# Loading x whole and gating on VectorE between the stages of a two-layer diffusion trunk on one Trainium2 core

## The chip, the cores and the metric

The kernel runs as one program on one core of a Trainium2 chip. The core's engines work side by side, each through its own list of instructions in a fixed order: TensorE (PE in the profile), VectorE (DVE), ScalarE (ACT), GpSimd (POOL), and SyncE (SP), which here issues the DMA transfers. An engine that has to wait for another holds up everything behind the waiting instruction in its own list. The metric is the device time of one execution in microseconds; lower is better.

## The reference, cut to what matters

The computation is two layers of a hybrid trunk over 640 tokens: 128 context tokens and 512 latent tokens, each of 1024 channels. What concerns the change is the end of each half of a layer:

```python
mix = (ga * ya + gb * yb + gc * yc) @ lp['w_o']
x = x + gt1 * rms_norm(mix, lp['g_post1'])

h2 = rms_norm(x, lp['g_pre2']) * (1 + sc2) + sh2
ffn = (jax.nn.silu(h2 @ lp['w_gate']) * (h2 @ lp['w_up'])) @ lp['w_down']
x = x + gt2 * rms_norm(ffn, lp['g_post2'])
```

So twice in a layer a product is normed over the channels (`rms_norm` divides by the root of the mean square), multiplied by a gate, and added to x; then x is normed again, scaled and shifted, and goes into the next products. The gate, scale and shift of a channel differ between context and latent tokens.

## The kernel before, in words

Activations lie with channels on the 128 partitions and tokens along the row: x is eight tiles (k = 0 to 7) of 128 by 640. Work on them is done in two halves of 320 tokens, h = 0 and h = 1. Half 0 holds all 128 context tokens and 192 latent ones, so a factor per channel needs two pieces there, of 128 and 192 columns (`SEGS`); half 1 is all latent and needs one piece of 320.

Products are in float32 by three matmuls: each operand is split into a high and a low part, and high by high, high by low and low by high are added up in PSUM. An item is one output block of 128 channels for one half: 24 matmuls where eight k-blocks are summed. Weights come by DMA into three raw buffers (`wraw`, 256 KB); ScalarE casts the high part (`wkh`, `whi`, `wk`; line 94) and VectorE subtracts it to get the low part (`wkl`, `wlo`, `wk`; line 95). A raw buffer is free again when VectorE's subtraction is done.

Four boundaries use `lin_res` (lines 459 to 510). I call them A (after w_o in layer 0), B (after w_down in layer 0, ahead of layer 1), C (after w_o in layer 1) and D (after w_down in layer 1, the end). At each:

1. Items of the product finish. For each, ScalarE squares the result into `sqt` (line 148), the squares are summed in `acc` by GpSimd and VectorE (line 152), and ScalarE multiplies the result by the gate into `y` (line 474; at B and D the tile is called `pt`, as it already holds a part of the sum, which VectorE adds first in line 471).
2. A matmul with ones (`ln`, line 157) sums `acc` over the channels, and ScalarE makes the factor `rs` by a logarithm and an exponential (lines 130 and 131).
3. For each k VectorE multiplies y by `rs` (line 498) and adds x (line 499). x was stored in memory and comes back in half tiles `xo` (line 496), which have three buffers. At D it already comes back whole (`xe`).
4. The squares of the new x are summed again: ScalarE squares, GpSimd adds k = 1 to 5, VectorE adds k = 6 and 7 (line 152); a second matmul with ones (`pn`) and a second `rs` follow.
5. `prenorm_apply` makes the next activations, a high and a low tile for each k (`h2h`/`h2l` at A and C, `hh`/`hl` at the start and at B). Half 0 does it in five instructions: VectorE multiplies by `rs` (line 175) and scales and shifts 128 columns (line 180), ScalarE does the other 192 (line 182) and casts the high part (line 183), VectorE subtracts (line 184). Half 1 needs three: VectorE (187), ScalarE (188), VectorE (189). The same function runs at the start of the kernel.

While this goes on for half 0, TensorE works on the items of half 1; while it goes on for half 1, TensorE works on the first items of the next stage with half 0's activations. The weights of both are kept, so each is split once. A scheduler sets the order of each engine's list before the run, from the program's dependences. Results of TensorE wait in three PSUM banks of the kind `l`; an item's bank is free when it has been read out, which at A and C for the gate item of the next stage means ScalarE's `fs` and VectorE's copy `fg` (line 429).

Of the kernel before, what the change touches and what calls it, by code (L numbers as in the profile page):

```python
# [8 lines left out]
F32 = mybir.dt.float32  # L9
F32R = mybir.dt.float32r  # L10
AF = mybir.ActivationFunctionType
ALU = mybir.AluOpType
AX = mybir.AxisListType

P = 128
# [15 lines left out]
NL, NB = 3, 5  # L31
NH_, NC_, NF_, NT_ = 16, 24, 16, 4
NWR, NW = 3, 3
NXO, NRR, NVW = 3, 3, 2

KEEP = ("C", "C", "C", "C", "E", None)
LEAD = ("C", "C", "C", "C", "E")
F1 = 14
# [14 lines left out]
def tile_trunk(ctx: ExitStack, tc: tile.TileContext, I: dict, O: list, layers=DEPTH):  # L53
# [7 lines left out]
    def slot(name, shape=(P, NT), dt=F32, tag="F"):  # L61
        n = {"H": NH_, "C": NC_, "F": NF_}[tag]
        return sb.tile(list(shape), dt, tag=tag, name=name, bufs=n)
# [2 lines left out]
        return slot(name, shape, dt, "C")  # L66

    def half(name, tag="T"):
        return sb.tile([P, HF], F32, tag=tag, name=name, bufs={"T": NT_, "acc": 3, "rs": 2, "xo": NXO}[tag])

    def lbank():
        return pp.tile([P, 512], F32, tag="l", name="l", bufs=NL)
# [7 lines left out]
    def hv(t, h):  # L80
        return t[:, h * HF:(h + 1) * HF]
# [86 lines left out]
    def prenorm_apply(src, h, r, gs, sh, hh, ks=range(KD)):  # L168
        for k in ks:
            if k:  # L170
                yield
            hi, lo = hh[k]
            t = half("hv")
            if h == 0:
                V.tensor_mul(t, hv(src[k], h), r)
                f = half("hf")
                for c0, c1, s in SEGS[h]:
                    g_, s_ = gs[:, k, s:s + 1], sh[:, k, s:s + 1]
                    if s:
                        V.tensor_scalar(out=f[:, c0:c1], in0=t[:, c0:c1], scalar1=g_, scalar2=s_, op0=ALU.mult, op1=ALU.add)  # L180
                    else:
                        A.activation(f[:, c0:c1], t[:, c0:c1], AF.Identity, scale=g_, bias=s_)
                A.copy(hv(hi, h), f)
                V.tensor_sub(hv(lo, h), f, hv(hi, h).bitcast(F32))
                continue
            s = 0
            V.scalar_tensor_tensor(out=t, in0=hv(src[k], h), scalar=gs[:, k, s:s + 1], in1=r, op0=ALU.mult, op1=ALU.mult)
            A.activation(hv(hi, h), t, AF.Identity, bias=sh[:, k, s:s + 1])
            V.scalar_tensor_tensor(out=hv(lo, h), in0=t, scalar=sh[:, k, s:s + 1], in1=hv(hi, h).bitcast(F32),
                                   op0=ALU.add, op1=ALU.subtract)  # L190

    def prenorm_half(src, h, gs, sh, hh):
        accs = prenorm_sum(src, h)
# [251 lines left out]
    def copy_ev(dst):  # L445
        def ev(h, pb):
            A.copy(hv(dst, h), pb)  # L447
        return ev

    def hslots(name, tag):  # L450
        return [(slot(f"{name}h{k}", dt=F32R, tag=tag), slot(f"{name}l{k}", dt=F32R, tag=tag)) for k in range(KD)]

# [3 lines left out]
        for k in range(KD):  # L456
            SY.dma_start(out=xd[k], in_=src[k])

    def lin_res(srcw, acts, ys, gs, keeps, part, after, end=False):

        accs = [[], []]
        n0 = KD - len(keeps)

        def ev(m):
            def f(h, pb):
                src = pb
                if part:
                    src = hv(ys[m], h)  # L470
                    V.tensor_add(src, src, pb)
                sumsq(accs[h], src, NSQ[m])
                for c0, c1, s in SEGS[h]:
                    A.mul(ys[m][:, c0:c1], src[:, c0 - h * HF:c1 - h * HF], gs[:, m, s:s + 1])
            return f

        def w(m):
            return srcw[:, m * P:(m + 1) * P]

        for m in range(n0):  # L480
            linear(w(m), acts, ev(m))
        bl = [wblocks(w(n0 + i), len(acts), k) for i, k in enumerate(keeps)]

        if end:
            xe = [slot("xe", tag="H") for _ in range(KD)]
            for k in range(KD):
                SY.dma_start(out=xe[k], in_=xd[k])

        def norm(h):
            r = half_rstd(accs[h], "ln")  # L490
            for k in range(KD):
                if end:
                    xo = hv(xe[k], h)
                else:
                    xo = half("xo", "xo")
                    SY.dma_start(out=xo, in_=hv(xd[k], h))
                E_ = G if end and k in ENDG else V
                E_.tensor_mul(hv(ys[k], h), hv(ys[k], h), r)
                E_.tensor_add(hv(ys[k], h), hv(ys[k], h), xo)
            yield from after(h)  # L500

        side = iter(())
        for h in range(2):
            for i, b in enumerate(bl):
                lin_half(b, acts, h, ev(n0 + i))
                next(side, None)
            drain(side)
            side = norm(h)
            next(side, None)
        return side  # L510
# [757 lines left out]
    for l in range(layers):  # L1268
# [33 lines left out]
        def fillc():  # L1302
# [8 lines left out]
            while len(yf) < 4:  # L1311
# [9 lines left out]
        ys = [cslot(f"y{k}") for k in range(KD)]  # L1321
        h2 = hslots("h2", "H")
        side = lin_res(I["w_o"][l], mix, ys, gsc[l][1], KEEP, False,
                lambda h: prenorm_half(ys, h, gsc[l][2], modT[l][:, 24:32, :], h2))
        mods = iter(())
        if l + 1 < layers:
            drain(load_rows(l + 1))
# [10 lines left out]
        if l + 1 < layers:  # L1338
            hh = hslots("h", "H")
            after = lambda h: prenorm_half(part, h, gsc[l + 1][0], modT[l + 1][:, 0:8, :], hh)  # L1340
        else:
            after = lambda h: out_half(part, h)
        side = lin_res(I["w_down"][l, F1 * P:], acts2, part, gsc[l][3], KEEP, True, after, l + 1 == layers)
        xs = part

    drain(side)
# [61 lines left out]
```

## Time and profile before

| | |
|---|---|
| median of 3 runs | 2819.4 us (2819.39 to 2822.23) |
| the profiled execution | 2820.49 us, of which the span is 2818.6 us |
| PE busy | 2724.1 us, 97% of the span |
| DVE busy | 1554.2 us, 55% |
| ACT busy | 1250.4 us, 44% |
| POOL busy | 114.2 us, 4% |
| mean granted clock of TensorE | 0.987 of full speed |

An engine's busy time is how long its instructions ran, overlaps counted once. With TensorE busy for 97% of the span, the time can only fall where TensorE waits or runs at a lower clock, and it rises wherever a change makes TensorE wait longer.

### The profile page before, as it was taken

The page shows a single profiled execution, that of the slowest core. Times are in us where ns is not written, and L with a number is a line of the kernel's source. Part 1 is how long each engine was busy: PE and PEld are TensorE (multiplying, and loading weights), DVE is VectorE, ACT ScalarE, POOL GpSimd, SP SyncE. Part 2 cuts the span into 40 slices and gives each one's busy share as a digit, 9 for nine tenths or more (in the row PEclk, how much of TensorE's full clock was granted, in tenths as well). Part 3 has the DMA queues.
Part 4 walks back from the last instruction along what each step waited for, and adds up shares of the span by engine and source line. Part 5 has one row for each costly group of instructions (what it writes and reads, how often), then busy time and mean ns, then how long its engine had stood idle before and what let it go on. Part 6 is the DMA issues. An engine that isn't in the chain of part 4 may idle for free.

```text
span 2818.6 us, 49773 instructions
## 1 busy us (share of the span) xinstructions
PE 2724.1 (97%) x19706; PEld 2594.3 (92%) x19706; DVE 1554.2 (55%) x3275; ACT 1250.4 (44%) x2863; POOL 114.2 (4%) x235
## 2 busy tenths in 40 slices
PE   7899999999999999999989999999999999999998
PEld 3898999999899899999978899999999989999997
DVE  4586566478743744324465865664778456442344
ACT  4432554466534533223455335434655354332333
POOL 1000000000001200000020000000000020000002
PEclk9999999999999999999999999999999999999999
DMA  8452355433464444444443323433233332222231
GB/s 244 77 85 46 79 100 117 85 71 84 155 161 137 146 132 144 128 159 143 132 115 75 78 49 79 104 98 82 65 98 118 94 108 92 76 74 77 75 119 64
DMA packets 401557, 293.45 MB, mean 104 GB/s; under 512 B 19318, under 2 KB 365228, under 8 KB 401324
## 3 DMA queue, kind: packets, MB, share of 16 engines
q1 hardware_dynamic: 401324, 290.28, 40.1%
q8 instruction: 154, 2.52, 0.3%
q14 instruction: 79, 0.65, 0.1%
HBM read 257.10 MB, written 33.11 MB: 103 GB/s over the span
## 4 chain that ended last, share of the span: by engine, by line
PE 78%; DVE 8%; DMA 8%; ACT 3%; issue 2%; SPq 0%; POOL 0%; DVEq 0%; ACTq 0%; POOLq 0%
PE l L363 21%; PE l L364 21%; PE l L365 21%; DMA rowb<-gd 3%; DMA wraw<-in_w_in_dram 2%; PE pm L324 1%; DVE wlo L95 1%; PE ptT L772 1%; PE po L782 1%; DVE tmpE L987 1%; DVE Tt L989 1%; PE sco L363 1%; DMA wm<-in_w_mod_dram 1%; PE scan L1068 1%; PE po L784 1%
## 5 line engine op out<-in xcount | busy, mean ns | idle before, releaser
L94 ACT CAST whi<-wraw 128x512 fp32r<-128x512 f32 (+1 forms) x540 | 331.2, 614 | 849.6 <-PE l L364 787.1
L95 DVE TENSOR_TENSOR wlo<-wraw,whi 128x512 fp32r<-128x512 f32 (+1 forms) x540 | 368.9, 684 | 537.4 <-ACT whi L94 507.8
L363 PE MATMUL l<-hh,whi 128*128 128x320 f32 x1856 | 592.0, 319 | 21.3 <-ACT padc L864 10.5
L365 PE MATMUL l<-hh,wlo 128*128 128x320 f32 x1856 | 584.4, 315 | 1.0 <-DVE wlo L95 1.0
L364 PE MATMUL l<-hl,whi 128*128 128x320 f32 x1856 | 584.4, 315 | 0.0
L363 PE MATMUL l<-h2h,whi 128*128 128x320 f32 x1248 | 387.7, 311 | 0.0
L364 PE MATMUL l<-h2l,whi 128*128 128x320 f32 x1248 | 385.7, 309 | 0.0
L365 PE MATMUL l<-h2h,wlo 128*128 128x320 f32 x1248 | 385.6, 309 | 0.0
L363 PEld LDWEIGHTS l<-hh,whi 128*128 128x128 f32 x1856 | 353.3, 190 | 28.9 <-ACT padc L864 11.8
L365 PEld LDWEIGHTS l<-hh,wlo 128*128 128x128 f32 x1856 | 353.4, 190 | 2.2 <-DVE wlo L95 1.2
L364 PEld LDWEIGHTS l<-hl,whi 128*128 128x128 f32 x1856 | 353.2, 190 | 2.1
L363 PEld LDWEIGHTS l<-h2h,whi 128*128 128x128 f32 x1248 | 234.6, 188 | 7.0 <-ACT fs L427 3.1
L364 PEld LDWEIGHTS l<-h2l,whi 128*128 128x128 f32 x1248 | 234.7, 188 | 0.0
L365 PEld LDWEIGHTS l<-h2h,wlo 128*128 128x128 f32 x1248 | 234.6, 188 | 0.0
L363 PE MATMUL l<-ah,whi 128*128 128x320 f32 x544 | 169.1, 311 | 0.0
L152 POOL TENSOR_TENSOR acc<-acc,sqt 128x320 f32<-128x320 f32 x88 | 88.1, 1001 | 1985.2 <-ACT sqt L148 1983.4
L365 PE MATMUL l<-ah,wlo 128*128 128x320 f32 x544 | 168.1, 309 | 0.0
L364 PE MATMUL l<-al,whi 128*128 128x320 f32 x544 | 167.9, 309 | 0.0
L363 PE MATMUL l<-rsh,whi 128*128 128x320 f32 x384 | 119.4, 314 | 0.0
L364 PE MATMUL l<-rsl,whi 128*128 128x320 f32 x384 | 118.4, 312 | 0.0
L365 PE MATMUL l<-rsh,wlo 128*128 128x320 f32 x384 | 118.2, 310 | 0.0
L363 PEld LDWEIGHTS l<-ah,whi 128*128 128x128 f32 x544 | 102.2, 188 | 2.2 <-ACT pt L447 1.7
(428 smaller groups left out, 5420.4 us busy)
## 6 DMA issues: line engine op xcount, KB each, us to landing
wraw<-in_w_in_dram SPq DMA_DIRECT2D x256, 256.0 KB, 4.3
wm<-in_w_mod_dram SPq DMA_DIRECT2D x80, 512.0 KB, 4.8
wraw<-in_w_gate_dram SPq DMA_DIRECT2D x88, 256.0 KB, 2.9
wraw<-in_w_up_dram SPq DMA_DIRECT2D x88, 256.0 KB, 3.1
wraw<-in_w_down_dram SPq DMA_DIRECT2D x80, 256.0 KB, 2.8
rowb<-gd SPq DMA_DIRECT2D x32, 320.0 KB, 9.4
mixo<-mixd SPq DMA_DIRECT2D x32, 320.0 KB, 3.4
wm<-in_w_mod_dram SPq DMA_DIRECT2D x32, 256.0 KB, 3.9
```

Of the source, the lines that this page charges most:

```text
L94: A.copy(hi, src)
L95: V.tensor_sub(lo, src, hi.bitcast(F32))
L152: (V if n == 2 else G).tensor_add(accs[0], accs[0], t)
L324: T.matmul(pm[32 * u:32 * u + 2, 0:256], lhsT=sc[:, k, :], rhs=w[:, u * 256:(u + 1) * 256], start=(n == 0), stop=(n == KD - 1))
L363: T.matmul(out, lhsT=wh, rhs=ah, start=first, stop=False)
L364: T.matmul(out, lhsT=wh, rhs=al, start=False, stop=False)
L365: T.matmul(out, lhsT=wl, rhs=ah, start=False, stop=last)
L772: T.transpose(pt[:, i, q * P:(q + 1) * P], sm_[q][:, kt * P:(kt + 1) * P], ident)
L782: T.matmul(po, lhsT=vh, rhs=th, start=(kt == 0), stop=False)
L784: T.matmul(po, lhsT=vh, rhs=tl, start=False, stop=(kt == 4))
L987: V.tensor_tensor(out=tv, in0=Tt[:, j + 1:32, j:j + 1].to_broadcast([P, n, j]), in1=Tt[:, j:j + 1, 0:j].to_broadcast([P, n, j]), op=ALU.mult)
L989: V.tensor_add(Tt[:, j + 1:32, 0:j], Tt[:, j + 1:32, 0:j], tv)
```

## The change

Three edits, all between the stages:

- x is loaded whole (eight transfers of 128 by 640) into the high tiles of the next activations, which are empty until `prenorm_apply` writes them; the half tiles `xo` are gone. The loads are issued right behind those of the kept weights.
- The gate is no longer applied when an item is read out. ScalarE only copies the product (or does nothing at B and D, where VectorE has already added it in place), and VectorE applies gate and `rs` in one instruction with a scalar and two tensors. Half 0 needs two of them per k (128 and 192 columns). At the end GpSimd keeps its two tiles in the old form.
- `prenorm_apply` has one form: VectorE scales by gain and `rs`, ScalarE adds the shift into the high tile, VectorE makes the low tile, each once per piece.

```diff
-            if h == 0:
-                V.tensor_mul(t, hv(src[k], h), r)
-                f = half("hf")
...
-                A.copy(hv(hi, h), f)
-                V.tensor_sub(hv(lo, h), f, hv(hi, h).bitcast(F32))
-                continue
...
+            for c0, c1, s in SEGS[h]:
+                a, b = c0 - h * HF, c1 - h * HF
+                V.scalar_tensor_tensor(out=t[:, a:b], in0=src[k][:, c0:c1], scalar=gs[:, k, s:s + 1], in1=r[:, a:b],
+                                       op0=ALU.mult, op1=ALU.mult)
+                A.activation(hi[:, c0:c1], t[:, a:b], AF.Identity, bias=sh[:, k, s:s + 1])
+            for c0, c1, s in SEGS[h]:
+                a, b = c0 - h * HF, c1 - h * HF
+                V.scalar_tensor_tensor(out=lo[:, c0:c1], in0=t[:, a:b], scalar=sh[:, k, s:s + 1],
+                                       in1=hi[:, c0:c1].bitcast(F32), op0=ALU.add, op1=ALU.subtract)
...
-                for c0, c1, s in SEGS[h]:
-                    A.mul(ys[m][:, c0:c1], src[:, c0 - h * HF:c1 - h * HF], gs[:, m, s:s + 1])
+                if end and m in ENDG:
+                    for c0, c1, s in SEGS[h]:
+                        A.mul(ys[m][:, c0:c1], src[:, c0 - h * HF:c1 - h * HF], gs[:, m, s:s + 1])
+                elif not part:
+                    A.copy(hv(ys[m], h), src)
...
-        if end:
-            xe = [slot("xe", tag="H") for _ in range(KD)]
-            for k in range(KD):
-                SY.dma_start(out=xe[k], in_=xd[k])
+        for k in range(KD):
+            SY.dma_start(out=xe[k], in_=xd[k])
...
-                if end:
-                    xo = hv(xe[k], h)
-                else:
-                    xo = half("xo", "xo")
-                    SY.dma_start(out=xo, in_=hv(xd[k], h))
-                E_ = G if end and k in ENDG else V
-                E_.tensor_mul(hv(ys[k], h), hv(ys[k], h), r)
-                E_.tensor_add(hv(ys[k], h), hv(ys[k], h), xo)
+                y = hv(ys[k], h)
+                if end and k in ENDG:
+                    G.tensor_mul(y, y, r)
+                    G.tensor_add(y, y, hv(xe[k], h))
+                    continue
+                for c0, c1, s in SEGS[h]:
+                    V.scalar_tensor_tensor(out=ys[k][:, c0:c1], in0=ys[k][:, c0:c1], scalar=gs[:, k, s:s + 1],
+                                           in1=r[:, c0 - h * HF:c1 - h * HF], op0=ALU.mult, op1=ALU.mult)
+                V.tensor_add(y, y, hv(xe[k], h))
```

The change also moves instructions in the engines' lists. Three places matter. The first is VectorE at boundary C, half 0, where the last tiles of step 3 stand (`y6`, `y7`; `wkl` are weight splits of the next stage; `acc` gets the last two squares of step 4). Before:

```order
L498 TENSOR_TENSOR y7_25071<-y7_25071,rs_25480 128x320
L499 TENSOR_TENSOR y5_25069<-y5_25069,xo_25503 128x320
L95 TENSOR_TENSOR wkl_25847<-wraw_25844,wkh_25846 128x512
L95 TENSOR_TENSOR wkl_25853<-wraw_25850,wkh_25852 128x512
L499 TENSOR_TENSOR y6_25070<-y6_25070,xo_25507 128x320
L499 TENSOR_TENSOR y7_25071<-y7_25071,xo_25511 128x320
L95 TENSOR_TENSOR wkl_25859<-wraw_25856,wkh_25858 128x512
L152 TENSOR_TENSOR acc_25515<-acc_25515,sqt_25532 128x320
```

and now:

```order
L497 SCALAR_TENSOR_TENSOR y7_25007<-y7_25007,gsc1_1_300,rs_25416 128x128
L499 TENSOR_TENSOR y6_25006<-y6_25006,h2h6_25020 128x320
L497 SCALAR_TENSOR_TENSOR y7_25007<-y7_25007,gsc1_1_300,rs_25416 128x192
L95 TENSOR_TENSOR wkl_25759<-wraw_25756,wkh_25758 128x512
L499 TENSOR_TENSOR y7_25007<-y7_25007,h2h7_25022 128x320
L152 TENSOR_TENSOR acc_25443<-acc_25443,sqt_25460 128x320
L95 TENSOR_TENSOR wkl_25765<-wraw_25762,wkh_25764 128x512
L152 TENSOR_TENSOR acc_25443<-acc_25443,sqt_25463 128x320
```

Two weight splits stood ahead of the last x additions and one stands there now; another has come between the two sums. A k takes two gate instructions and an addition where it took two.

The second place is the same engine at C, half 1. `fg` is VectorE's reading of the first gate item of the next stage (bank `l`), `wlo` are weight splits. Before:

```order
L498 TENSOR_TENSOR y7_25071<-y7_25071,rs_25775 128x320
L429 COPY fg_25839<-l_25902 128x320
L95 TENSOR_TENSOR wlo_26227<-wraw_26224,whi_26226 128x512
L499 TENSOR_TENSOR y5_25069<-y5_25069,xo_25798 128x320
L499 TENSOR_TENSOR y6_25070<-y6_25070,xo_25802 128x320
L1174 TENSOR_TENSOR fs_25838<-fs_25838,fg_25839 128x320
L95 TENSOR_TENSOR wlo_26233<-wraw_26230,whi_26232 128x512
L499 TENSOR_TENSOR y7_25071<-y7_25071,xo_25806 128x320
L152 TENSOR_TENSOR acc_25810<-acc_25810,sqt_25827 128x320
```

and now:

```order
L497 SCALAR_TENSOR_TENSOR y7_25007<-y7_25007,gsc1_1_300,rs_25703 128x320
L499 TENSOR_TENSOR y6_25006<-y6_25006,h2h6_25020 128x320
L499 TENSOR_TENSOR y7_25007<-y7_25007,h2h7_25022 128x320
L422 COPY fg_25751<-l_25814 128x320
L152 TENSOR_TENSOR acc_25722<-acc_25722,sqt_25739 128x320
L1174 TENSOR_TENSOR fs_25750<-fs_25750,fg_25751 128x320
L152 TENSOR_TENSOR acc_25722<-acc_25722,sqt_25742 128x320
```

The x additions now run without the next stage's work among them, and the copy that frees a PSUM bank has moved behind all of them. On TensorE the fourth item of the next stage, which needs that bank, had 18 of its 24 matmuls ahead of `pn`, and has 8 now. At A the lists have moved in the same way.

The third place is ScalarE at B, half 0, around the second factor (`rs` of `pn`). Before:

```order
L474 ACTIVATE pt2_12816<-pt2_12816,gsc0_3_298 128x320
L130 ACTIVATE rs_15544<-pn_15542,eps_68 128x320
L94 CAST wkh_15890<-wraw_15888 128x512
L131 ACTIVATE rs_15544<-rs_15544 128x320
L94 CAST wkh_15896<-wraw_15894 128x512
L182 ACTIVATE hf_15579<-hv_15577,modT1_294,gsc1_0_299 128x192
```

and now:

```order
L94 CAST wkh_15814<-wraw_15812 128x512
L130 ACTIVATE rs_15502<-pn_15500,eps_68 128x320
L94 CAST wkh_15820<-wraw_15818 128x512
L131 ACTIVATE rs_15502<-rs_15502 128x320
L148 ACTIVATE sqt_15567<-pt3_12793 128x320
L179 ACTIVATE hh0_15042<-hv_15534,modT1_294 128x128
```

Before, the casts of the fourth and fifth weight block of the next stage stood on both sides of the exponential; now it is the third block alone, and the fourth stands six rows further on, behind the first activations.

## Rows read from the trace of the kernel before

**Rows 1.** The page, part 1: busy time, share of the span, instructions.

```profile
PE 2724.1 (97%) x19706; PEld 2594.3 (92%) x19706; DVE 1554.2 (55%) x3275; ACT 1250.4 (44%) x2863; POOL 114.2 (4%) x235
```

**Rows 2.** Waits of PE at A, B, C, D: waiter, releaser, us in total, times, longest.

```profile
PE pn L157 <- DVE acc L152: 4.8, 2, 4.0
PE l L363 <- DVE fg L429: 1.7, 1, 1.7
...
PE pn L157 <- DVE acc L152: 5.9, 2, 3.0
PE l L813 <- ACT hh L183: 2.1, 2, 1.6
...
PE pn L157 <- DVE acc L152: 6.5, 2, 4.1
...
PE yt L1236 <- DVE pt L499: 7.2, 5, 3.9
```

**Rows 3.** Timeline of DVE at C, half 0: start, duration, instruction, count, idle before.

```profile
2295.61 0.90 DVE L498 TENSOR_TENSOR y<-y,rs 128x320 f32<-128x320 f32 x2 [8.21 <-ACT rs L131]
...
2299.25 1.16 DVE L499 TENSOR_TENSOR y<-y,xo 128x320 f32<-128x320 f32 x1
...
2303.30 2.64 DVE L95 TENSOR_TENSOR wkl<-wraw,wkh 128x512 fp32r<-128x512 f32 x2
2305.86 0.88 DVE L499 TENSOR_TENSOR y<-y,xo 128x320 f32<-128x320 f32 x2
...
2307.27 1.65 DVE L152 TENSOR_TENSOR acc<-acc,sqt 128x320 f32<-128x320 f32 x2
```

**Rows 4.** Timeline of DVE at C, half 1.

```profile
2326.60 0.49 DVE L498 TENSOR_TENSOR y<-y,rs 128x320 f32<-128x320 f32 x1
...
2334.78 0.48 DVE L429 COPY fg<-l 128x320 f32<-128x320 f32 x1
...
2338.25 1.15 DVE L499 TENSOR_TENSOR y<-y,xo 128x320 f32<-128x320 f32 x1
...
2340.12 0.48 DVE L152 TENSOR_TENSOR acc<-acc,sqt 128x320 f32<-128x320 f32 x1
...
2343.04 1.47 DVE L187 SCALAR_TENSOR_TENSOR hv<-y,gsc,rs 128x320 f32<-128x320 f32 x3
```

**Rows 5.** Busy time of PE, PEld, DVE, ACT, POOL by stretch, PEclk, DMA.

```profile
2309.80:2314.50 4.70, 4.70 (x18) 4.50 (x17) 3.47 (x7) 4.25 (x10) 1.13 (x1) 0.50 0.59 163
2314.70:2322.90 8.20, 8.20 (x58) 8.20 (x57) 6.63 (x13) 6.37 (x15) 3.09 (x3) 1.00 0.20 57
```

**Rows 6.** The chain of waits through B: start, duration, piece.

```profile
1424.81 4.79 DMA xo<-xd
...
1436.42 4.92 DMA wraw<-in_w_in_dram
...
1456.60 4.09 DMA xo<-xd
...
1472.61 0.81 PE pn L157 x2
```

**Rows 7.** Timeline of DVE at B: first and last tile of half 0's activations.

```profile
1440.62 0.48 DVE L175 TENSOR_TENSOR hv<-pt,rs 128x320 f32<-128x320 f32 x1
...
1460.32 0.49 DVE L184 TENSOR_TENSOR hl<-hf,hh 128x320 fp32r<-128x320 f32 x1 [1.01 <-ACT hh L183]
```

**Rows 8.** Instructions of DVE by form, whole span: count, busy us, mean ns.

```profile
L954 DVE SCALAR_TENSOR_TENSOR Dt<-rowb,kc,cst 128x128 f32<-128x128 f32 x80 | 23.1, 347 | 31.3 <-DMA rowb<-gd 31.1
...
L189 DVE SCALAR_TENSOR_TENSOR h2l<-hv,modT,h2h 128x320 fp32r<-128x320 f32 x16 | 8.3, 546 | 0.2 <-ACT h2h L188 0.2
```

**Rows 9.** Line 499's waits for a transfer, whole span: us, times.

```profile
  DMA xo<-xd: 2.6, 2
```

**Rows 10.** Timeline of ACT near the start of the kernel.

```profile
77.85 0.62 ACT L94 CAST whi<-wraw 128x512 fp32r<-128x512 f32 x1 [2.49 <-DMA wraw<-in_w_in_dram]
```

**Rows 11.** DMA issues between 2730 and 2760 us: count, KB each, us to landing.

```profile
xe<-xd SPq DMA_DIRECT2D x8, 320.0 KB, 4.4
```

More of the change, by code (lines that the diff above doesn't have):

```diff
@@ L33 @@
 NWR, NW = 3, 3
-NXO, NRR, NVW = 3, 3, 2
+NRR, NVW = 3, 2
 KEEP = ("C", "C", "C", "C", "E", None)
@@ L68, in half @@
     def half(name, tag="T"):
-        return sb.tile([P, HF], F32, tag=tag, name=name, bufs={"T": NT_, "acc": 3, "rs": 2, "xo": NXO}[tag])
+        return sb.tile([P, HF], F32, tag=tag, name=name, bufs={"T": NT_, "acc": 3, "rs": 2}[tag])
     def lbank():
@@ L173, in prenorm_apply @@
             t = half("hv")
-            if h == 0:
-                V.tensor_mul(t, hv(src[k], h), r)
-                f = half("hf")
-                for c0, c1, s in SEGS[h]:
-                    g_, s_ = gs[:, k, s:s + 1], sh[:, k, s:s + 1]
-                    if s:
-                        V.tensor_scalar(out=f[:, c0:c1], in0=t[:, c0:c1], scalar1=g_, scalar2=s_, op0=ALU.mult, op1=ALU.add)
-                    else:
-                        A.activation(f[:, c0:c1], t[:, c0:c1], AF.Identity, scale=g_, bias=s_)
-                A.copy(hv(hi, h), f)
-                V.tensor_sub(hv(lo, h), f, hv(hi, h).bitcast(F32))
-                continue
[L186 to L190, printed above, removed]
+            for c0, c1, s in SEGS[h]:
[7 more added lines that the diff above has]
+                                       in1=hi[:, c0:c1].bitcast(F32), op0=ALU.add, op1=ALU.subtract)
     def prenorm_half(src, h, gs, sh, hh):
@@ L448, in copy_ev, with f32_of @@
         return ev
+    def f32_of(hh):
+        return [hi.bitcast(F32) for hi, _ in hh]
     def hslots(name, tag):
@@ L457, in store_x, with lin_res @@
             SY.dma_start(out=xd[k], in_=src[k])
-    def lin_res(srcw, acts, ys, gs, keeps, part, after, end=False):
+    def lin_res(srcw, acts, ys, gs, keeps, part, after, xe, end=False):
         accs = [[], []]
@@ L472, in f @@
                 sumsq(accs[h], src, NSQ[m])
-                for c0, c1, s in SEGS[h]:
-                    A.mul(ys[m][:, c0:c1], src[:, c0 - h * HF:c1 - h * HF], gs[:, m, s:s + 1])
+                if end and m in ENDG:
[3 more added lines that the diff above has]
+                    A.copy(hv(ys[m], h), src)
             return f
@@ L1323, in tile_trunk @@
         side = lin_res(I["w_o"][l], mix, ys, gsc[l][1], KEEP, False,
-                lambda h: prenorm_half(ys, h, gsc[l][2], modT[l][:, 24:32, :], h2))
+                       lambda h: prenorm_half(ys, h, gsc[l][2], modT[l][:, 24:32, :], h2), f32_of(h2))
         mods = iter(())
@@ L1340, in tile_trunk @@
             after = lambda h: prenorm_half(part, h, gsc[l + 1][0], modT[l + 1][:, 0:8, :], hh)
+            xe = f32_of(hh)
         else:
             after = lambda h: out_half(part, h)
-        side = lin_res(I["w_down"][l, F1 * P:], acts2, part, gsc[l][3], KEEP, True, after, l + 1 == layers)
+            xe = [slot("xe", tag="H") for _ in range(KD)]
+        side = lin_res(I["w_down"][l, F1 * P:], acts2, part, gsc[l][3], KEEP, True, after, xe, l + 1 == layers)
         xs = part
```

1 line of the change is left out of this document (removed).

## The prediction

> **What bounds the kernel now.** I read the page first. TensorE is busy for 97% of the span, no other engine for more than 55% [rows 1]; so only what TensorE waits for counts. The table of TensorE's waits at the four boundaries comes next [rows 2]. The reader is to see that at A, B and C nearly all of its waiting is for `pn`, the matmul that needs the last square sum from VectorE: 4.8, 5.9 and 6.5 us, each in two waits, one per half, and that at the end (D) it is 7.2 us for the x addition of line 499. All that is in reach here is about 30 us, 1% of the time; a change of 0.2% (5.6 us, about what a measurement of this kernel tells from no change) needs a fifth of it. Then VectorE's timeline inside two of these waits [rows 3, 4] says what the chain to `pn` is made of. At B the chain of waits shows transfers as well [rows 6].
>
> **Prices.** Two adjacent additions or multiplications of 128x320 take 0.90 us and one 0.49 [rows 3, 4], so one costs 0.41 in a queue. The three-operand form of 128x320 takes 0.546 alone and three take 1.47 [rows 4, 8], so 0.46 in a queue, 0.08 less than alone. Of 128x128 one takes 0.347 [rows 8], so 0.27; between them, by columns, 192 columns take 0.41 alone and 0.33 in a queue. The gate with `rs` thus costs 0.60 per k in half 0 where the product cost 0.41, and 0.46 in half 1. Eight k with their additions: 8 x 1.01 = 8.1 us against 8 x 0.82 = 6.6 in half 0 (+1.5), 7.0 against 6.6 in half 1 (+0.4).
>
> **Holds by GpSimd.** An addition that alone takes 0.48 takes 1.16 at 2299.25 [rows 3]; two more read like it, and the pair of splits at 2303.30 takes 2.64 where two take 1.3. That is five holds of 0.68, 3.4 us, one for each of the five sums that GpSimd makes in this stretch. The change leaves these five. Whether a three-operand instruction is held in the same way no row shows. From below: not held at all, then two in three of these instructions escape, 2.3 us less in half 0. From above: each of the two pieces of a k is held once for one GpSimd sum, five more holds. I take the same five, as the held additions are the nearest row.
>
> The Trainium skill, SBUF — State Buffer, section "Who interferes with whom", says that a VectorE instruction with two SBUF inputs contends with a GpSimd instruction that reads SBUF. The held additions at 2299.25 agree [rows 3]. By that rule the three-operand form, which has two such inputs, is held too, so the sum stays as below; without it the first rival's price would come.
>
> **ScalarE** loses its multiplication at B and D, and has a copy for it at A and C. TensorE waits for neither in [rows 2], since the three banks cover it: 0, from below -1.
>
> **Boundary C, half 0.** Before: from 2295.61, 6.6 of work, 1.2 for two splits, 3.4 of holds; the last addition ends at 2306.74 and the second sum at 2308.92 [rows 3]. After: 8.1, one split of 0.6 and 3.4, plus 0.1 for the last one's own length, so the last addition ends at 2307.8. Behind it a sum (0.4), a split (0.6) and the last sum (0.48) end at 2309.3, or 2310.0 if the last one is held as before (1.65 for two). That is 0.4 to 1.1 later. TensorE does three more matmuls before it stands at `pn`; at 0.141 each (8.20 us for 58 [rows 5]) these 0.4 us lie inside the wait. Net 0 to +0.7; I take +0.3. The wait is followed, as before, by a stretch at the granted clock 0.50, the 1.2 GHz level, where a matmul takes 0.261 (4.70 us for 18 [rows 5]); 18 matmuls cost 2.2 us more there than at full clock. I leave that as it is.
>
> **Boundary C, half 1.** Before: from 2326.60 the chain runs among other work (half 0's last low tiles, the copy `fg`, splits) until the second sum ends at 2340.6 [rows 4]. TensorE had reached `pn` 2.4 us earlier (6.5 less 4.1 [rows 2]), at 2338.2, and its fourth item 18 matmuls, 2.5 us, before that, at 2335.7; the copy of 2334.78 had freed the bank by then [rows 4]. After: 7.0 of work and 3.4 of holds, nothing between; the additions end at 2337.0, and the copy, now behind them, at 2337.4. TensorE waits 1.7 us at the fourth item, a wait that is not there before, runs 8 matmuls (1.1) and is at `pn` at 2338.5, when the second sum has just ended (copy, sum, product, sum: 4 x 0.41 from 2337.0). It is two microseconds ahead on the clock and ten matmuls (1.4) behind in work: -0.6. The next half item is 40 matmuls long, 5.6 us, and covers `rs` and the first activations, as the 30 before did. C together: -0.3.
>
> **Boundary A.** The same order and the same two parts, with +0.3 in half 0. In half 1 the two waits are 0.8 (`pn`) and 1.7 (`fg` [rows 2]), 2.5 in all. The x wait goes (0.8, the smaller of the two in line 499's 2.6 [rows 9]), and the copy still comes behind the additions: about 2.2, so -0.3. A together: 0. Here the eight whole loads stand among the weight loads of w_o. At D the same loads are in the kernel already: eight of 320 KB, 4.4 us each [rows 11], and TensorE waits there only for VectorE. So nothing for them, from above 4.4 us if one blocks a weight.
>
> **Boundary B.** Half 0: the chain has a wait of 1.8 us for x (2.6 less 0.8 [rows 9]), which the chain of waits shows as a transfer of 4.79 [rows 6]. It goes and the three-operand pieces bring 1.5: the sum comes out even. Then the second factor. A weight transfer from 1436.42 to 1441.34 [rows 6] holds a cast that stands on ScalarE ahead of the first activation, and another cast stands ahead of the exponential. After, only a block loaded long before stands there. The first tile starts at 1440.62 before [rows 7]; after I put it at 1439.2. Eight k of 1.19 us (two pieces scaled 0.60, two made low 0.60), with three splits (1.8), four additions of product parts (1.6) and four holds (2.7) end at about 1455.0, and with a last split at 1455.6, where the last low tile now starts at 1460.32 [rows 7]. The second half's product with x then runs without its x transfer (4.09 from 1456.60 [rows 6]): from 1456, 7.0 + 3.4 = 10.4 us, to 1466.4, and two sums with splits end at 1467.8 where `pn` now starts at 1472.61: 4.8 us earlier. TensorE has 8 matmuls (1.1) fewer behind it at that point, so -3.7. The two waits for `hh` (2.1 [rows 2]) are inside this and are not counted again. From below -5; from above -1, if the fourth weight, whose raw buffer is now freed behind the last sum and not before it, comes too late.
>
> **D and the start.** D already has whole loads. Half 0 hides behind product items; in half 1 the six VectorE tiles cost 6 x 0.05 more, and the first already moves the wait of line 1236: +0.2. At the start the norm's half 0 costs VectorE 1.2 instead of 1.1 us per k and ScalarE less, and a split moves behind half 1; but ScalarE waits for a weight until 77.85 whatever comes before [rows 10]. 0, from -0.5 to +2.
>
> **Sum.** 0 (A) - 3.7 (B) - 0.3 (C) + 0.2 (D) + 0 = -3.8 us. The profiled execution took 2820.5, so 2816.7; it lies 1.1 above the median of the runs, 2819.4, so the forecast is 2815.6.
>
> **Rivals.** *The holds go (or most waits with them).* If the three-operand form is not held, each half 0 at A, B and C is 2.3 us shorter, each half 1 about 1.0 (a half of the instructions, and the copy behind them), and D 1.0: 10.9 on top of 3.8, 14.7; where a wait has gone nothing more can be saved, as at the `pn` wait of 0.8 at A's half 1, so I put -13: 2806.4. For it: no such instruction is seen held. Against it: the additions are [rows 3].
>
> *Slower: half 0's pieces lengthen the chain straight into `pn`.* At A and C TensorE already waits there [rows 2], so each microsecond on VectorE is one of the kernel's. If both pieces of a k are held, half 0 costs 1.5 more in work and 2 to 3 more holds (1.4 to 2.0) at A and C, some 3.2 each, and at B as much, which eats 3.2 of the 3.7 there; with 0.5 in each half 1: +3.2 x 3 + 1.5 - 3.8 = +7; 2826.5. It decides from two extra holds per half on. For it: only one instruction in the chain has become cheaper, none is gone. Against: GpSimd makes five sums however VectorE is cut.
>
> *The x waits were hidden anyway.* They sum to 2.6 us in two places [rows 9]; if B's late activations come from the weights alone, the raw buffers free no sooner, and B gives 1 and not 3.7: -1; 2818.4.
>
> **How the numbers follow.** The forecast 0.50 (its own range 2811.5 to 2819), holds gone 0.20, slower 0.15, hidden anyway 0.15. Of the forecast's half, a third goes past 5.6 us: 0.17 + 0.20 = 0.37 faster. Slower: 0.13 of the 0.15. The rest, 0.50, is within 0.2%. The range 2807 to 2823 leaves out the ends of the two outer cases.
>
> **What would show it.** Right: no wait for `xo`; at B `pn` of half 1 near 1468 on a span shifted by what goes before; at C and A a wait for `fg` of 1.5 to 2.5 us in place of most of half 1's `pn` wait, and half 0's `pn` wait of 4 to 5 us; held three-operand instructions (a 128x192 of about 1.1 us). Wrong: three-operand instructions that stay short beside GpSimd; a wait of TensorE for weights at A; a gain spread over A and C rather than at B.

## The result and the profile after

The changed kernel takes 2837.93 us (median of 5 runs, 2832.89 to 2845.86) against 2822.13 us for the kernel before, run beside it (2819.39 to 2823.55). The ratio is 1.0058, with a 95% interval of 1.0045 to 1.0071: slower by some 16 us. The forecast was 2815.6, its range 2807 to 2823. Three far longer executions of the kernel before, among those beside the experiments (3720.69, 4348.85 and 6681.34 us), are left out of every ratio and spread.

Both kernels give TensorE 19706 matmuls, in the same order but for places moved by a few matmuls. So the n-th matmul of one profile can be set against the n-th of the other, at places between the moved ones. The profiled executions took 2839.12 and 2820.49 us. The first line of the table is the time of before; the second is how much longer TensorE takes for that stretch after the change:

| start to 230 | 230 to 850 | A, 850 to 970 | to 1400 | B, to 1490 | behind B, to 1660 | to 1880 | to 2270 | C, to 2365 | rest |
|---|---|---|---|---|---|---|---|---|---|
| +6.5 | 0.0 | +4.1 | -0.1 | -0.6 | +5.2 | +0.9 | +3.1 | -0.1 | +0.3 |

The sum is 19.3 us; the tail behind the last matmul is 0.7 shorter. For the first and the third the forecast was 0, for the sixth it had no term. One execution of each kernel was profiled, and a stretch can come out some 5 us longer in one execution: the kernel with the start undone (below) shows +5.2 from 230 to 850, where its waits are no longer than before.

**The clock.** The page of the changed kernel, part 1:

```profile
PE 2733.6 (96%) x19706; PEld 2603.7 (92%) x19706; DVE 1563.2 (55%) x3337; ACT 1225.0 (43%) x2805; POOL 112.2 (4%) x235
```

Against [rows 1] TensorE is busy 9.5 us longer with the same number of matmuls, and its mean granted clock is 0.983 where it was 0.987. So only half of the 18.6 us by which the profiled span grew is waiting; the other half is matmuls that run slower, in stretches at the lower level of the clock (granted 0.50, as in the first line of [rows 5]). Over the five executions of the changed kernel the mean granted clock is 0.981 to 0.985, lowest in the longest.

**The boundaries.** TensorE's waits in the changed kernel, which answer to [rows 2] (waiter, releaser, us in total, times, longest), at A with the modulation weights ahead of it, at B, at C and at D:

```profile
PE l L356 <- ACT y L475: 3.6, 1, 3.6
PE l L356 <- DVE fg L422: 3.5, 1, 3.5
PE pm L317 <- DMA wm<-in_w_mod_dram: 2.3, 2, 1.3
PE ln L157 <- ACT sqt L148: 1.1, 1, 1.1
PE ln L157 <- POOL acc L152: 0.7, 1, 0.7
...
PE pn L157 <- DVE acc L152: 3.8, 2, 3.3
PE l L356 <- DVE pt L469: 2.3, 1, 2.3
PE l L813 <- ACT hh L179: 1.5, 1, 1.5
...
PE l L356 <- ACT y L475: 3.6, 1, 3.6
PE l L356 <- DVE fg L422: 2.9, 1, 2.9
...
PE yt L1236 <- DVE pt L499: 7.6, 3, 4.6
```

No wait for `xo` is left. At A and C the waits for `pn` have gone too, but the same time is spent one item earlier: in half 0 at a bank that ScalarE's copy `y` should have emptied, and that copy stands behind the squares of the new x, so it comes as late as VectorE's chain; in half 1 at the bank of `fg`. A new wait of 2.3 us is for the modulation weights. In the window that the first five lines are from (870 to 970), which starts earlier than that of [rows 2], the kernel before also waits 1.0 us for ScalarE's `y` and 0.2 for a weight: 7.7 us in all, against 11.2 now.

VectorE's three-operand instructions are held by GpSimd. Its timeline in the changed kernel (start, duration, instruction, count) at A, half 0 and then half 1, answering to [rows 3, 4]:

```profile
921.63 1.92 DVE L497 SCALAR_TENSOR_TENSOR y<-y,gsc,rs 128x192 f32<-128x192 f32 x2
...
923.88 0.67 DVE L497 SCALAR_TENSOR_TENSOR y<-y,gsc,rs 128x192 f32<-128x192 f32 x2
...
928.11 1.01 DVE L497 SCALAR_TENSOR_TENSOR y<-y,gsc,rs 128x192 f32<-128x192 f32 x1
...
954.37 2.25 DVE L497 SCALAR_TENSOR_TENSOR y<-y,gsc,rs 128x320 f32<-128x320 f32 x2
```

Two pieces of a k take 0.67 us free and 1.92 held, a single one of 192 columns 1.01 held, two of 320 columns 2.25 where two take 1.01 elsewhere in the same queue.

**B** shows what came in place of the x wait. VectorE, then GpSimd, then ScalarE at the end of B's half 1, after the change:

```profile
1473.78 0.88 DVE L499 TENSOR_TENSOR pt<-pt,hh 128x320 f32<-128x320 f32 x2
...
1478.87 0.49 DVE L152 TENSOR_TENSOR acc<-acc,sqt 128x320 f32<-128x320 f32 x1 [3.60 <-POOL acc L152]
```

```profile
1469.44 1.87 POOL L152 TENSOR_TENSOR acc<-acc,sqt 128x320 f32<-128x320 f32 x1 [11.19 <-ACT sqt L148]
1473.39 5.44 POOL L152 TENSOR_TENSOR acc<-acc,sqt 128x320 f32<-128x320 f32 x4 [2.08 <-ACT sqt L148]
```

```profile
1472.26 0.62 ACT L94 CAST whi<-wraw 128x512 fp32r<-128x512 f32 x1 [2.00 <-DMA wraw<-in_w_in_dram]
1472.78 1.55 ACT L148 ACTIVATE sqt<-pt 128x320 f32<-128x320 f32 x4
```

VectorE has added the last x at 1474.66, splits a weight, and then stands for 3.60 us: its own sums go into the same `acc` as GpSimd's five, and those are not done. In the kernel before VectorE did not wait for GpSimd in this half. GpSimd is late for two reasons. ScalarE's squares stand behind a cast that waits 2.00 us for its weight block, so GpSimd has nothing to add for 2.08. And two of its sums take longer than the 0.87 of the last three: the first 1.87 and, of the four from 1473.39 on, the first 2.61.

**The start.** VectorE around the end of the first norm, in the changed kernel:

```profile
66.58 1.47 DVE L182 SCALAR_TENSOR_TENSOR hl<-hv,modT,hh 128x320 fp32r<-128x320 f32 x3
67.96 0.68 DVE L95 TENSOR_TENSOR wkl<-wraw,wkh 128x512 fp32r<-128x512 f32 x1
...
69.17 0.68 DVE L95 TENSOR_TENSOR wkl<-wraw,wkh 128x512 fp32r<-128x512 f32 x1
```

All three weight subtractions that free raw buffers stand behind the last low tile. In the kernel before, one stood among the tiles at 57.18. SyncE's issues in the changed kernel, and then in the kernel before:

```profile
53.82 0.38 SPq L367 DMA_DIRECT2D wraw<-in_w_in_dram  x1
...
68.72 0.38 SPq L367 DMA_DIRECT2D wraw<-in_w_in_dram  x1
69.31 13.49 SPq L352 DMA_DIRECT2D wraw<-in_w_in_dram  x6
```

```profile
54.96 0.37 SPq L374 DMA_DIRECT2D wraw<-in_w_in_dram  x1
...
59.12 0.68 SPq L359 DMA_DIRECT2D wraw<-in_w_in_dram  x1
```

The weight load issued at 54.96 before is issued at 68.72 after. ScalarE, in the changed kernel, then casts the blocks as they land (in brackets the idle time before, and what ended it):

```profile
73.05 0.62 ACT L94 CAST wk<-wraw 128x512 fp32r<-128x512 f32 x1 [5.22 <-DMA wraw<-in_w_in_dram]
77.40 0.62 ACT L94 CAST whi<-wraw 128x512 fp32r<-128x512 f32 x1 [3.73 <-DMA wraw<-in_w_in_dram]
...
81.06 0.62 ACT L94 CAST whi<-wraw 128x512 fp32r<-128x512 f32 x1 [0.49 <-DMA wraw<-in_w_in_dram]
...
81.92 0.42 ACT L815 COPY lg<-l 128x320 f32<-128x320 f32 x1
```

The last of these casts starts at 81.06 and not at 77.85 as in [rows 10], `lg` 3.5 us later (78.37 before). TensorE's wait for `dz`, which follows, is 4.0 us where it was 0.7, but others are shorter, and its waits from 60 to 135 sum to 9.9 us where they were 8.5. Most of the 6.5 us is the clock:

```profile
0.00:230.00 230.00, 201.05 (x1279) 168.44 (x1279) 134.38 (x310) 96.67 (x246) 14.57 (x56) 0.96 0.60 128
```

```profile
0.00:236.50 236.50, 206.02 (x1278) 171.97 (x1278) 135.76 (x318) 94.96 (x246) 14.54 (x56) 0.94 0.60 123
```

These are the same matmuls before and after but for one at the edge, columns as in [rows 5]: TensorE is busy 5.0 us longer with them, at a granted clock of 0.94 where it was 0.96.

**Behind B.** ScalarE, in the changed kernel and then in the kernel before, at the first gating tile of layer 1:

```profile
1510.57 0.21 ACT L959 ACTIVATE egl<-rowb 128x5 f32<-128x5 f32 x1 [1.62 <-DMA rowb<-gd]
1510.68 0.72 ACT L431 ACTIVATE zs<-zs 128x640 f32<-128x640 f32 x1
```

```profile
1499.40 0.73 ACT L438 ACTIVATE zs<-zs 128x640 f32<-128x640 f32 x1
...
1500.98 0.21 ACT L959 ACTIVATE egl<-rowb 128x5 f32<-128x5 f32 x1 [0.85 <-DMA rowb<-gd]
```

The scheduler has swapped them: `egl`, which waits for a transfer, now stands ahead of `zs`, for which VectorE waits. In the changed kernel TensorE then waits in this stretch for

```profile
PE l L356 <- ACT padc L864: 4.2, 2, 2.2
...
PE l L356 <- DVE cz L594: 1.5, 1, 1.5
PE nat L900 <- DVE dz L876: 1.4, 1, 1.4
```

where before it waited 2.6 us for `padc` and not for the other two: 4.5 us. No run takes this out by itself, but the other profiles agree with it: only the changed kernel and the one with the start undone have `egl` first, and this stretch is 5.2 and 5.3 us longer in them; in the other eleven `egl` stands behind, and the stretch lies between 4.1 shorter and 2.1 longer than before. One of the eleven is the changed kernel with its sums moved to VectorE, at 0.4.

### The profile page after: what moved, and what is told of

The parts are those of the page before. It is cut to its first block, busy times and chain, and to the rows that moved or that the text cites. A ratio compares the mean times of both kernels' runs of the same rounds, so it can differ in the third digit from the quotient of the medians.

```text
span 2837.2 us, 49702 instructions
## 1 busy us (share of the span) xinstructions
PE 2733.6 (96%) x19706; PEld 2603.7 (92%) x19706; DVE 1563.2 (55%) x3337; ACT 1225.0 (43%) x2805; POOL 112.2 (4%) x235
## 4 chain that ended last, share of the span: by engine, by line
PE 79%; DVE 9%; DMA 7%; ACT 3%; issue 2%; SPq 0%; POOL 0%; ACTq 0%; DVEq 0%; POOLq 0%
PE l L356 22%; PE l L357 21%; PE l L358 21%; DMA rowb<-gd 3%; DMA wraw<-in_w_in_dram 2%; PE pm L317 1%; DMA wm<-in_w_mod_dram 1%; DVE y L497 1%; PE ptT L772 1%; PE po L782 1%; PE sco L356 1%; DVE wlo L95 1%; DVE hv L177 1%; DVE Dt L954 1%; PE scan L1068 1%
```

## The experiments

All times are medians; the kernel before, run beside each group, gave 2822.2, 2823.4 and 2822.8. Its single runs spread over 10 to 14 us, so differences under 3 us between kernels are not leaned on.

**The start, undone.** The changed kernel, with half 0's five-step norm kept in the call at the start:

```
...
-    drain(prenorm_apply(xs, h, ..., range(4 * p, 4 * p + 4)))
+    drain(prenorm_apply(xs, h, ..., range(4 * p, 4 * p + 4), old=True))
```

> The changed kernel with the old five-step norm in half 0 at the start of the kernel alone (before layer 0); everything at the boundaries A to D as changed. Theory 'start': in the profile of the changed kernel the list of VectorE at the start has a weight split behind half 1's activations, so raw buffers come free 14 us later, two casts wait for their loads, and the chain to the transfers of the decays is late; 7 us of the 18.6 are lost between 65 and 138 us. Then this kernel is 6 to 8 us faster than the changed one (about 2830 to 2832) and its start reads as before. Rival 'boundaries': the loss comes from the longer VectorE chains at A to D, and the difference at the start is given back later; then it is within 2 us of the changed kernel (2836 to 2839).

Measured 2830.91, ratio to before 1.0034 [1.0021, 1.0047]: 7.0 us under the changed kernel, about what the table shows for the start, though the intervals just touch. Some 9 us remain. In its profile the weight load is issued at 54.67 again and `lg` is at 78.97, and the start is 4.0 us shorter than in the changed kernel. The wait for `dz` is still 3.1 us, so that wait is not what was won.

**The norm alone.** The kernel before, with `prenorm_apply` in its new form everywhere:

```
-            if h == 0:
-                V.tensor_mul(t, hv(src[k], h), r)
...
+            for c0, c1, s in SEGS[h]:
+                V.scalar_tensor_tensor(out=t[:, a:b], in0=src[k][:, c0:c1], scalar=gs[:, k, s:s + 1], ...)
```

> The kernel before with the three-step norm in half 0 alone (start and boundaries); gate on ScalarE, x in halves. Theory 'start': +7 at the start, near 0 at A, B, C; 2827 to 2831. Rival 'boundaries': 2832 or more if the pieces of the norm lengthen the chain there, or no more than 2824 if the start's loss is given back.

Measured 2829.6, ratio 1.003 [1.002, 1.004]. By the comparison of matmuls 6.1 of its loss lie ahead of 230 us.

**The gate alone.** The kernel before, with ScalarE's copy in place of its multiplication and this in `norm`, x still in halves:

```
+V.scalar_tensor_tensor(out=ys[k][:, c0:c1], in0=ys[k][:, c0:c1], scalar=gs[:, k, s:s + 1],
+                       in1=r[...], op0=ALU.mult, op1=ALU.mult)
 V.tensor_add(y, y, xo)
```

> The kernel before with the gate on VectorE alone (two pieces in half 0, one in half 1); the norm in five steps, x in halves. Theory 'start': no cost beyond the chain, 2820 to 2826, with the wait for pn at A and C longer by 0 to 1 us each. Rival 'boundaries' (both pieces held by GpSimd): +3 at each of A, B, C: 2829 to 2833, with held instructions of 128x192 near 1.1 us.

Measured 2823.13, ratio 0.9998 [0.9987, 1.001]: no difference beyond some 3 us. The gate's move is free.

**The whole loads alone.** The kernel before, with x loaded whole into the next high tiles:

```
+        for k in range(KD):
+            SY.dma_start(out=xe[k], in_=xd[k])
...
-                    xo = half("xo", "xo")
-                    SY.dma_start(out=xo, in_=hv(xd[k], h))
+                xo = hv(xe[k], h)
...
```

> The kernel before with x loaded whole into the next activations' high tiles alone; the gate on ScalarE, the norm in five steps. Theory 'whole loads cost at A': TensorE waits for the modulation weights near 880 us as in the changed kernel (1.3 and 1.0 us there), and B gains the 1.8 us of its x wait and more: 2817 to 2824, the two about even. Rival: the loads are what costs at A and behind B, 2827 or more.

Measured 2832.15, ratio 1.0036 [1.0023, 1.0049]: 9.9 us slower, as the rival had it, and the largest cost of the three. Its profile places 4.5 us at A, 1.8 at C, 3.8 between 1490 and 1880 and -1.2 at B. At A it shows why. GpSimd at A, half 1, in the kernel before and then with whole loads:

```profile
944.68 3.34 POOL L152 TENSOR_TENSOR acc<-acc,sqt 128x320 f32<-128x320 f32 x3 [9.00 <-ACT sqt L148]
949.41 2.15 POOL L152 TENSOR_TENSOR acc<-acc,sqt 128x320 f32<-128x320 f32 x2 [1.40 <-ACT sqt L148]
```

```profile
945.19 8.94 POOL L152 TENSOR_TENSOR acc<-acc,sqt 128x320 f32<-128x320 f32 x5 [8.68 <-ACT sqt L148]
```

Before, none of the five takes over 1.22 us. With whole loads the mean is 1.79, the figure in the expectations that follow, but the five are not alike. The first of them by itself:

```profile
945.19 5.18 POOL L152 TENSOR_TENSOR acc<-acc,sqt 128x320 f32<-128x320 f32 x1 [8.68 <-ACT sqt L148]
```

It takes 5.18 us and ends at 950.37, just behind VectorE's run of two-input instructions, whose last ends at 949.62; the other four take 0.86 each. VectorE, in the kernel before and then with whole loads:

```profile
945.70 0.49 DVE L499 TENSOR_TENSOR y<-y,xo 128x320 f32<-128x320 f32 x1 [0.80 <-DMA xo<-xd]
946.11 2.25 DVE L498 TENSOR_TENSOR y<-y,rs 128x320 f32<-128x320 f32 x2
```

```profile
946.53 0.88 DVE L495 TENSOR_TENSOR y<-y,rs 128x320 f32<-128x320 f32 x2
947.34 0.88 DVE L496 TENSOR_TENSOR y<-y,h2h 128x320 f32<-128x320 f32 x2
...
954.16 0.49 DVE L152 TENSOR_TENSOR acc<-acc,sqt 128x320 f32<-128x320 f32 x1 [4.53 <-POOL acc L152]
```

With x always there, VectorE's pairs take 0.88 us: it is not held at all. It is GpSimd that waits now, and VectorE has gained nothing, since it then waits 4.53 us for the sums. ScalarE stops as well, for want of a free square buffer:

```profile
950.40 0.47 ACT L148 ACTIVATE sqt<-y 128x320 f32<-128x320 f32 x1 [2.92 <-POOL acc L152]
```

and TensorE's wait in this half is a single one of 5.0 us for `pn`, where it was 0.8 and 1.7. The Trainium skill, SBUF — State Buffer, section "Who interferes with whom", says "Issue order, not op shape, decides who blocks." The two traces agree in that the same instructions in the same shapes have a different loser: a pair of VectorE's took 2.25 us at 946.11 before, with the x wait just ahead of it, and 0.88 at 946.53 here, where the sum took 5.18. Who issued first, no row shows.

So I had a theory: a sum on GpSimd starves while VectorE's two-input instructions come without a gap. The rival: eight more transfers among the weight loads, or `pn`'s place in TensorE's list, which the scheduler had moved 15 matmuls up at A. Three runs bear on this, and a fourth leaves the whole loads out.

**Whole loads at B alone.** `xe` is passed for w_down only; A and C keep `xo`:

```
-                modT[l][:, 24:32, :], h2), f32_of(h2))
+                modT[l][:, 24:32, :], h2), None)
```

> The kernel before with x loaded whole at boundary B alone (w_down of layer 0); at A and C x comes in halves as before. Theory one (starved sums): e4's 9.9 us come mostly from A and C, where without x waits VectorE's two-input instructions run back to back and GpSimd's sums take 1.79 us each instead of about 1.1; then this kernel is within 2 us of before, and with B's own gain a little faster: 2820 to 2823. Theory two (transfers): eight whole loads among weight loads delay TensorE wherever they stand, B and the blocks after it too; then a third to a half of the 9.9 is here: 2825 to 2827.

Measured 2819.88, ratio 0.9988 [0.9979, 0.9996]. The loads cost nothing at B; all of the 9.9 us comes with the loads at A and C. That is the side of theory one, but the run does not show starved sums to be the cause: at B, half 1, a sum takes 3.76 us here, and VectorE waits 4.56 us for `acc`, as long as with whole loads everywhere. Nor does it take whole loads: at A, half 0, where x comes in halves here, one sum takes 5.72 us.

**Whole loads, the sums on VectorE.**

```
-PSQ = (0, 0, 0, 0, 0, 0, 2, 2)
+PSQ = (0, 2, 2, 2, 2, 2, 2, 2)
```

> e4 (whole loads alone, 2832.15) with the squares of five of eight tiles in a half added on VectorE instead of GpSimd in the norm between the stages (PSQ 0,2,2,2,2,2,2,2). Starved sums: the sum at the end of a half no longer trails, pn's wait in A's half 1 falls from 5.0 us to about 2, A and C together 4 to 6 us shorter: 2826 to 2828. Rival, the transfers or pn's earlier place in TensorE's order make the loss: GpSimd's share is bought back by more work on VectorE (five sums of 0.41 us a half), so 2831 to 2835.

Measured 2814.85, ratio 0.9967 [0.9956, 0.9978]: 17.3 us under the whole loads alone, much more than I expected, and faster than the kernel before and the changed one. TensorE at A, with the same stretch as above:

```profile
PE l L363 <- ACT y L477: 2.8, 3, 1.5
PE pm L324 <- DMA wm<-in_w_mod_dram: 1.2, 2, 0.9
PE l L363 <- DVE fg L429: 0.9, 1, 0.9
PE pn L157 <- DVE acc L152: 0.5, 1, 0.5
```

VectorE in that half, in the same kernel:

```profile
945.50 0.89 DVE L495 TENSOR_TENSOR y<-y,rs 128x320 f32<-128x320 f32 x2
...
948.32 0.48 DVE L152 TENSOR_TENSOR acc<-acc,sqt 128x320 f32<-128x320 f32 x1
```

A sum costs VectorE 0.40 us in a queue. GpSimd's sum held a VectorE instruction for 0.68 us when it won [rows 3], and when it lost it trailed. Against the whole loads alone A is 7.9 us shorter and C 7.3. At C no sum had starved (none there took over 1.23 us); what moving them wins there is VectorE's holds (pairs of up to 2.27 us) and the wait for `fg`, which stood behind the x additions (3.6 us of TensorE's, now none). The 1.2 us wait for modulation weights stays; that part of the rival is real but small.

**The control.** The kernel before, with the same `PSQ`.

> Control for e6: the kernel before with the same sums on VectorE and x in halves. If GpSimd's sums are starved only where x never waits, this is level with or slower than before: 2821 to 2826. If moving the sums pays by itself, wherever x comes from, it is faster than before by as much as e6 is faster than e4: about 2817.

Measured 2817.82, ratio 0.9979 [0.997, 0.9988]. The expectation of no gain fell, and the time is where the rival put it: moving the sums pays 5.6 us by itself, and GpSimd's holds are in the kernel before too. With whole loads it pays 17.3. So whole loads cost 9.9 with the sums on GpSimd and nothing with the sums on VectorE. It is the sharing of the sums that makes them dear; how much of that is starved sums and how much holds and order, these runs don't separate.

**Gate and norm at the boundaries, without the whole loads and without the new start.** Against the changed kernel:

```
-                V.tensor_add(y, y, hv(xe[k], h))
+                V.tensor_add(y, y, xo)
...
+    drain(prenorm_apply(xs, h, ..., old=True))
```

> The two parts of the change without the whole loads: the gate on VectorE, and the three-step norm at A, B and C but the five-step one at the start. If the costs seen are those of the start (7.0 to 7.4) and of the whole loads (9.9), nothing is left: 2820 to 2824, and if the shorter norm helps C as in e2 (2.5 us there), 2819 to 2821. Rival: the three-step norm costs at the boundaries too, because the pieces lengthen VectorE's chain: 2825 or more.

Measured 2821.27, ratio 0.9993 [0.9983, 1.0002]: as before. These two parts cost nothing where they were meant to work. The kernel with the start undone (2830.91) differs from this one by the whole loads alone: 9.6 us, about what they cost without gate and norm.

**The changed kernel with the sums on VectorE** (the line `PSQ` as above), and **the same with the old start** (`PSQ` and `old=True`):

> The changed kernel as given, with the squares of five of eight tiles in a half added on VectorE instead of GpSimd in the norm between the stages. If trailing sums are what whole loads cost, e6 less e4 (17.3 us) goes from 2837.9, less what the gate's longer pieces take on the busier VectorE: 2820 to 2826. Rival, the gate with the factor lengthens VectorE's chain so far that more sums there only add: 2832 or more.

Measured 2826.49, ratio 1.0016 [1.0004, 1.0029]: 11.4 us under the changed kernel, just outside what I expected. By the profiles 4.8 of it lies behind B, where `egl` has gone back behind `zs`.

> As e9, and the five-step norm kept at the start alone. If the start's cost stands by itself, 7 us under e9: 2813 to 2819, that is faster than the kernel before by 4 to 10 us. Rival, the two costs overlap (one idle time was counted in both): within 3 us of e9.

Measured 2817.79, ratio 0.9992 [0.9981, 1.0003]: another 8.7, so the two costs stand beside each other. The start and the sums together take 20.1 us from the changed kernel; as moving the sums pays 5.6 in the kernel before too, 14.5 of the 15.8 us lost are accounted for by this reckoning. By its interval this kernel can't be told from before, and it lies 2.9 over the whole loads with the sums on VectorE, which lack the gate's and the norm's new forms.

**The start alone.** The kernel before, with the new norm in the call at the start only:

```
+    drain(prenorm_apply(xs, h, ..., range(4 * p, 4 * p + 4), new=True))
```

> The kernel before with the three-step norm at the start alone. If the whole of e2's 7.4 us is the start (the weight block's split behind half 1's tiles, so the next weight loads are issued 14 us later), 2828 to 2832. If the norm at the boundaries takes part in it, 2824 to 2826.

Measured 2827.84, ratio 1.0027 [1.0016, 1.0038]. By the median 5.0 us, on the edge below what I expected; by the ratio 7.6. The start costs something without any boundary changed; its size is 5 to 8 us.

**As the last but one** (sums on VectorE, old start), **but x in halves.** Against that kernel:

```
-                V.tensor_add(y, y, hv(xe[k], h))
+                V.tensor_add(y, y, xo)
```

> As e10 but x in halves (gate on VectorE, three-step norm at A, B and C, five-step norm at the start, sums on VectorE). If whole loads pay once the sums do not trail (e6 lies 3 us under e7), 3 us over e10: 2816 to 2822. Rival, they pay nothing or cost something with the gate beside them: equal to e10 or below it.

Measured 2824.17, ratio 1.0011 [1.0002, 1.002]: 2.2 above what I expected, and 6.4 over the same kernel with whole loads; between the two kernels with the old gate and norm the difference is 3.0 (2817.82 and 2814.85), too little to lean on alone. With the sums on VectorE whole loads cost nothing and, beside the new gate and norm, pay. This kernel differs from the one at 2821.27 by `PSQ` alone and is 2.9 slower: the 5.6 that moving the sums paid in the kernel before is not there beside the new gate and norm. With whole loads it paid in all three pairs: 17.3, 13.1 and 11.4.

## Why the prediction was wrong

- **The start**, "ScalarE waits for a weight until 77.85 whatever comes before", is the first step that failed. The wait is for a transfer, but the transfer is issued when VectorE's subtraction frees a raw buffer, and the new order put that subtraction behind both halves of the norm. Forecast 0, from -0.5 to +2; 7.0 us when undone (8.7 with the sums moved), 5 to 8 alone. I had noted that "a split moves behind half 1" and had put no price on the load that it releases. That the norm's form at the start costs this is shown by the runs; that it does so by the late load is read from the profiles, as no run moves that split alone.
- **The whole loads**, "nothing for them, from above 4.4 us", is the second. The blocked weight was there (2.3 us in the profile at A), but the larger cost was one that I had no term for: with the x waits gone, VectorE's instructions come without gaps, and a sum on GpSimd can stand until they end (5.18 us at A with the loads alone), so that VectorE waits for GpSimd. Alone the loads cost 9.9 us, and nothing once the sums are on VectorE. In the changed kernel this shows at B; at A the longest sum took 1.93 us, at C 1.30, and there VectorE is held instead.
- **B**, -3.7, gave -0.6. The chain on VectorE did what was forecast, and a little more: its last x addition ended at 1474.66, which less the 10.5 us by which the stretch begins later (the table's first four columns) is 1464.2 on the clock of before, against 1466.4 in my sum. It was held for 0.6 us there (a pair of 1.62 at 1470.51) and not for 3.4: this time GpSimd lost. Then came the 3.60 us for `acc`: `pn` starts 2.7 us earlier on the clock of before and not 4.8. I had counted how long GpSimd's sums hold VectorE, and never how long VectorE's instructions hold GpSimd. The 2.08 that GpSimd waited for its square come from a late weight on ScalarE, which stood in the forecast only as the bound of -1.
- **A and C.** C gave -0.1 where -0.3 was forecast, which is partly luck: TensorE's waits there grew from 6.9 to 8.1 us, and its matmuls took 1.2 us less, at a granted clock of 0.96 where it was 0.95. In half 1 the wait for `fg` came in place of the one for `pn`, as 2.9 and 3.5 us and not 1.5 to 2.5. That half 0's wait moved to ScalarE's copy `y` was not foreseen and changed nothing. "TensorE waits for neither" was read from [rows 2], whose window leaves out the 1.0 us for `y` at A. A's +4.1 against 0 is 3.5 of waits (11.2 against 7.7), 2.3 of them for the modulation weights, and the rest slower matmuls (granted clock 0.97 against 0.99).
- **The holds** were right: three-operand instructions are held like additions, and the rival that they escape is out. The gate cost nothing, as costed.
- **The slower rival** had the side and not the mechanism: it put the loss into the pieces of half 0, and the run of the gate alone shows none there.
- **The clock** behind the waits was to stay "as it is". In the profile TensorE's matmuls take 9.5 us longer than before. That is no cost beside the others but the form in which half of the loss comes, 5.0 us of it ahead of 230.
- **Behind B** nothing was forecast, and 5.2 us of the profiled difference lie there. The changed order of `egl` and `zs` accounts for 4.5 us of waits by the profile; no run takes it out by itself. The 3.1 us between 1880 and 2270, with a stretch at the granted clock 0.50 that no wait precedes in the profile, stay unexplained; the kernel with the new norm at the start alone shows the same 3.1 in its profile and the last kernel above, with the old start, 2.9, while the kernel with only the start undone shows none.

The parts measured singly add up to the whole: gate and norm at the boundaries -2.1, the start 5.0 to 7.4, the whole loads 9.9, together 12.8 to 15.2, against 15.8. By these runs the loss is the start and the whole loads; each carries several us of uncertainty.

## What to carry to other kernels

Taking a wait out of one engine's chain helps only if the engine that shares the work can follow: ask who else adds into the same tile, and what the waits had let it do. An instruction that frees a buffer is worth the transfer that it releases and not its own 0.6 us; when a change moves it, follow the buffer to the DMA's issue and to whoever waits for that. And if two engines get in each other's way, moving the shared chain onto one of them can beat both orders: here 40 sums went from GpSimd to the busier VectorE, and the kernel with whole loads went from 2832.15 to 2814.85. Without whole loads the same move paid 5.6 us in one kernel and nothing in another. A mean over a merged row hides such a contest: five sums of 1.79 were one of 5.18 and four of 0.86.

## What the runs showed of the hardware

The contest between VectorE and GpSimd goes either way. A 128x320 sum on GpSimd takes 0.86 to 0.88 us alone and up to 1.22 when it holds VectorE's additions to 2.25 a pair. When VectorE's instructions run on at 0.88 a pair, a sum can stand until the run has a gap and not only until the next instruction ends: 5.18 us at A with whole loads, 3.76 at B and 5.72 at A with whole loads at B alone. Three-operand instructions are held as additions are: the two pieces of a k take 0.67 us free and 1.92 held.
